# Moving the weight parts of the x-stationary products by 64 bytes, and one order for the products of all summed units

## Chip, cores and metric

The kernel runs on one core of one Trainium2 chip. The metric is device time in microseconds (us) of one execution, the median of the runs shown. Engines are named as the profile names them: PE (matrix products; PEld is its weight load), DVE and ACT (elementwise work), POOL and SP (here mostly issuing DMAs).

## The reference

Two layers over 256 tokens with 1024 features, all in float32. Each layer is a feed-forward block, a mixing block and a second feed-forward block; the first lines below are the whole of it.

```python
def swiglu(h, w_gate_up, w_down):
    a, b = jnp.split(h @ w_gate_up, 2, axis=-1)
    return (jax.nn.silu(a) * b) @ w_down

def hybrid_layer(x, ...):
    x = x + 0.5 * swiglu(rms_norm(x, ffn1_norm), ffn1_w_gate_up, ffn1_w_down)
    h = rms_norm(x, mix_norm)
    z = h @ w_in
    ...
    u, q, k, v, gl = z[..., :o1], z[..., o1:o2], z[..., o2:o3], z[..., o3:o4], z[..., o4:]
    ...
    merged = gates[:, :, 0] * (y_pool @ w_branch_pool) + gates[:, :, 1] * (y_attn @ w_branch_attn)
    x = x + merged @ w_out
    x = x + 0.5 * swiglu(rms_norm(x, ffn2_norm), ffn2_w_gate_up, ffn2_w_down)
    return x
```

y_pool is a causal pooling of u, and y_attn is attention over q, k and v. The sizes that matter: w_in has 4096 columns, the hidden width of a feed-forward block is 2816.

## The kernel before

**Parts and products.** A float32 product is made of three products of float32r parts: each operand is split into a high part, which ACT writes as a copy (lines 198, 209, 319), and a low part, which DVE writes as the difference (lines 199, 210, 320). High times high, high times low and low times high are added in PSUM; low times low is left out. `steps` (line 218) reorders the columns of the moving operand and of the output in pieces of 16 bytes.

**Units of weights.** All weights come as units of 128 x 2048 floats (1 MB). `fetch` (line 134) takes the next unit of a plan, issues its DMA on SP into one of four `raw` tiles, and has its two halves split into two `hi` and two `lo` tiles of 128 x 1024, from a pool with six buffers of each name (`buffers`, line 202). The unit then waits in a list until `unit` (line 128) hands it to the products.

**Weights stationary.** In most stages the weight block is the stationary operand and x, or what was made from x, moves: `chain` (line 228) multiplies a high weight block with the high and low x parts side by side (512 columns) and then the low weight block with the high x part (256 columns). `pair` (line 246) does this for one unit: eight blocks of features, two outputs, 32 products. The x parts are in the tile hx, one pair of 256 columns for each block of 128 features.

**x stationary.** Two places turn this round: a block of 128 features of x for 128 tokens is stationary, and the weights move.

- `tokens` (line 686) makes q, k and v: three calls in a layer, each over two units of w_in, and for each half of the tokens. For each block of features it does four products: high x with 512 high weight columns, high x with the first 256 low columns, low x with 512 high columns, and high x with the last 256 low columns. The stationary blocks are slices of hx.
- `by_tokens` (line 555) does the same for **summed units**. In three of the four feed-forward blocks (all but the very first) some products by the gate and up weights are made in Strassen's manner: seven products of sums of quadrants take the place of eight. Form 1 to 7 of a group A, B or C is called "1A", "7C" and so on. The sums of weights are formed in HBM beforehand by accumulating DMAs from POOL (`go_on`, line 175), loaded by `sum_form` (line 187) and split like any unit. Of x, forms 1, 2 and 4 use quadrants of hx themselves; forms 3, 5, 6 and 7 use sums of quadrants, which `x_forms` (line 525) makes and splits into the tile sf. Forms 1, 2 and 4 thus have slices of hx stationary, the others slices of sf.

Each summed unit is 16 products: four blocks of 128 features with four products each. A forms list, TWO or THREE (lines 54 and 56), is the order in which a feed-forward block takes plain units (numbers, each a `pair`), summed units and the transposes "t0A" and the like, which turn a finished result back. The first block after the mixing block of layer 0 uses TWO, the two feed-forward blocks of layer 1 use THREE. Runs of summed units, such as "4A", "2B", "3A", "7B", "6B" in THREE, follow one another without a `pair` between.

**The order of the work.** Products stay on PE in the order in which the code writes them (`keep`, line 107). In `by_tokens` the four products of a block are written in two ways: for forms 3, 5, 6 and 7 as in `tokens` (512, 256, 512, 256 columns), for forms 1, 2 and 4 as 512, 512, 256, 256.

**Addresses.** A tile's place follows from the sizes of those ahead of it. In the program before, all `hi` and `lo` tiles begin at 32 modulo 128 bytes, and so do hx, ga, gb, gc and gd (the moving operands of the feed-forward blocks). Only the parts in sf begin 64 bytes further (SHIFT is 16 floats, line 49; `eight`, line 396), at 96 modulo 128. A block's own offsets are multiples of 512 bytes.

Of the kernel before, what the change touches and what calls it, by code (L numbers as in the profile page):

```python
# [19 lines left out]
F32R = mybir.dt.float32r  # L20
# [5 lines left out]
P = 128  # L26
# [5 lines left out]
NF = DFF // P  # L32
# [6 lines left out]
HALF = 8 * P  # L39
# [6 lines left out]
LU = FU + NF + NF // 2  # L46
GROUPS = {"A": 12, "B": 8, "C": 18}
XF = 2
SHIFT = 16
# [29 lines left out]
def trunk_kernel(ctx: ExitStack, tc: tile.TileContext, x_in, w_in, pw_in, qkn_in, rope_in, mask_in, band_in, out):  # L79
# [4 lines left out]
    parts = ctx.enter_context(tc.tile_pool(name="parts", bufs=6))  # L84
# [24 lines left out]
    def mm(*args, **kw):  # L109
        return keep(nc.tensor.matmul(*args, **kw))  # L110
# [17 lines left out]
    def unit():  # L128

        if not ahead:  # L130
            fetch()
        return ahead.pop(0)

    def fetch(last=None):

        u = next(plan)
        if isinstance(u, tuple):
            ahead.append(sum_form(*u))
            return
        raw, hi, lo = buffers()  # L140
        n = HALF if u < 4 else 2 * HALF
        for c in range(0, 2 * HALF, n):
            nc.sync.dma_start(raw[:, c:c + n], w_in[u, :, c:c + n])
        for h in range(2):
            low = split(raw[:, h * HALF:(h + 1) * HALF], hi[h], lo[h])
        if last:
            behind(low, last)
        ahead.append((hi, lo))
# [3 lines left out]
    def quadrant(base, g, q):  # L152

        n, kh = base + GROUPS[g] + (0 if q[1] == "1" else 2), int(q[0]) - 1
        return w_in[n:n + 2, :, kh * HALF:(kh + 1) * HALF].rearrange("u p c -> p u c")

    def two_rows(z):
        return z.rearrange("p (i c) -> p i c", i=2)
# [28 lines left out]
    def sum_form(base, n):  # L187

        f, g = n
        z, hi, lo = buffers()  # L190
        src = quadrant(base, g, RAW[f]) if f in RAW else two_rows(far.pop((f, g, base)))
        z = two_rows(z)
        nc.sync.dma_start(z, src)
        z = z.rearrange("p i (k c) -> p i k c", c=2 * P)
        for h in range(2):
            a = z[:, :, 2 * h:2 * h + 2, :]
            hv, lv = (t[h].rearrange("p (k i c) -> p i k c", i=2, c=2 * P) for t in (hi, lo))
            act(hv, a, AF.Copy)  # L198
            tt(lv, a, hv.bitcast(F32), op=OP.subtract)  # L199
        return hi, lo  # L200

    def buffers():
        raw = raws.tile([P, 2 * HALF], F32, name="raw", tag="raw")
        hi = [parts.tile([P, HALF], F32R, name="hi", tag="hi") for _ in range(2)]
        lo = [parts.tile([P, HALF], F32R, name="lo", tag="lo") for _ in range(2)]
        return raw, hi, lo

    def split(w, hi, lo):
        act(hi, w, AF.Copy)  # L209
        return tt(lo, w, hi.bitcast(F32), op=OP.subtract)  # L210

    def blk(z, b, n=1):

        size = z[0].shape[-1]
        c = b * P % size
        return z[b * P // size][:, c:c + n * P]

    def steps(z):

        if len(z.shape) == 3:  # L220
            z = z.rearrange("p a s -> p (a s)")
        return z.rearrange("p (s a c) -> p a s c", a=4, c=4)

    def prod(ps, w, xk, first, last, **kw):

        return mm(steps(ps), lhsT=w, rhs=steps(xk), start=first, stop=last, **kw)
# [35 lines left out]
    def behind(z, other):  # L262

        tc.add_manual_dep(z.ins, other.ins.name, mybir.DependencyInfo(
            mybir.DependencyClass.NoSync, mybir.DependencyReason.DATA), reason="behind")
# [130 lines left out]
    def eight(dtype, name, at=0):  # L396
        z = acts.tile([P, NK * GW + 4 * SHIFT], dtype, name=name, tag="gates")[:, at:]
        return [z[:, i * GW:(i + 1) * GW] for i in range(NK)]
# [21 lines left out]
    def ffn(after, n0=0, end=False, col=None, base=0, far_at=(), steps_at=()):  # L420
        gs, gt = {}, {}

        def room(name, n0, m):
            g = acts.tile([P, m, 2, S], F32R, name=name, tag=name)
            gt[name] = g
            gs.update({n0 + i: g[:, i] for i in range(m)})
# [9 lines left out]
        abs_, more = {}, []  # L436
# [40 lines left out]
        if n0:  # L477
            room("gb", 16, NF - 16)
            ws = [unit() for _ in range(n0)]
            pairs(ws, [wide(n) for n in range(n0)])  # L480
            pair(unit(), wide(n0), sums, NK // 2)
            fetch()
            done = 0
            for i in range(n0 + 1, NF + 1):
                if i < NF:
                    pair(unit(), wide(i))
                    fetch()
                    if i in (7,9,11,13,15,17,19,21):
                        go_on()
                if i == NF or i % 3 != 1:  # L490
                    for n in range(done, NF if i == NF else min(done + 2, i - 1), 2):
                        scaled = post(n)
                        done = n + 2
                        if i == n0 + 1:
                            behind(scaled, drained[-1])
        else:
# [24 lines left out]
            sf = {}  # L521
# [3 lines left out]
            def x_forms():  # L525

                late = drained[-1]
                for k in range(NK):
                    behind(act(xg[:, k, :], x[:, k, :], AF.Copy, scale=gain[:, l_of[0], col + k:col + k + 1]), late)
                (a11, a21), (a12, a22) = ([z[:, :, t * P:(t + 1) * P] for t in range(2)] for z in (xg[:, :4], xg[:, 4:]))  # L530
                s1, s2 = (pre[:, (8 + 2 * i) * S:(10 + 2 * i) * S].rearrange("p (k s) -> p k s", s=P) for i in range(2))
                s3, s4 = (vt[:, i, :].rearrange("p (k s) -> p k s", s=P) for i in range(2))
                fs = iter(eight(F32R, "sf", SHIFT))

                def parts_of(n, z):
                    sh, sl = (next(fs).rearrange("p (k s) -> p k s", s=P) for _ in range(2))
                    act(sh, z, AF.Copy)
                    tt(sl, z, sh.bitcast(F32), op=OP.subtract)
                    sf[n] = [(sh[:, k, :], sl[:, k, :]) for k in range(4)]

                tt(s3, a11, a21, op=OP.subtract)
                parts_of("7", s3)
                yield
                tt(s1, a22, a21, op=OP.subtract)
                stt(s2, s1, -1.0, a11, op0=OP.mult, op1=OP.subtract)
                parts_of("6", s2)
                yield
                parts_of("5", s1)
                yield
                stt(s4, s2, -1.0, a12, op0=OP.mult, op1=OP.subtract)  # L550
                parts_of("3", s4)
                room("gb", 16, NF - 16)
                yield

            def by_tokens(f, ps, first):

                hi, lo = unit()
                more = {} if first else {"skip_group_check": True}
                for k, (ah, al) in enumerate(sf[f]):
                    wh, wl = blk(hi, 4 * k, 4), blk(lo, 4 * k, 4)  # L560
                    low = ps[:, :S], ah, wl[:, :S], False, False
                    prod(ps, ah, wh, first and k == 0, False, **more)
                    if f not in "124":
                        prod(*low, **more)
                    prod(ps, al, wh, False, False, **more)
                    if f in "124":
                        prod(*low, **more)
                    prod(ps[:, S:], ah, wl[:, S:], False, k == 3, **more)
                fetch()

# [23 lines left out]
            def seven(f, g):  # L594

                z = bank[f + g]
                p1, w = tk[g][:, 0], tk[g][:, 1]
                if f == "5":
                    if g == "B":
                        gated(p1, 0, 0, 0)  # L600
                    if three and g == "C":
                        p1 = tk["B"][:, 0]
                by_tokens(f, z, f in "127")
                if f == "1":
                    act(p1, z, AF.Copy)
                elif f == "2":
                    tt(p1, z, p1, op=OP.add)
                    if g != "B":
                        gated(p1, 0, 0, 0)
                elif f == "6":  # L610
                    act(w, z, AF.Copy)
                elif f == "5":
                    act(p1, z, AF.Copy)
                    tt(p1, bank["7" + g], p1, op=OP.add)
                    gated(p1, 1, 1, 1)
                elif f == "3":
                    gated(z, 0, 1, 1)
                elif f == "4":
                    tt(w, z, w, op=OP.add)
                    gated(w, 1, 0, 0)  # L620
# [5 lines left out]
            for n in FEED[base][2:]:  # L626
# [4 lines left out]
                n, t = n if isinstance(n, tuple) else (n, None)  # L631
# [16 lines left out]
        for f, k in order:  # L648
            u, c = divmod(f * NF + k, 16)
# [4 lines left out]
            hi, lo = parts_of[u]  # L654
# [382 lines left out]
    for f in range(0, NK, 2):  # L1037
# [3 lines left out]
        for u, (raw, hi, lo) in enumerate(w3):  # L1041
            nc.sync.dma_start(raw[:, 2 * f * P:2 * (f + 2) * P], w_in[u, :, 2 * f * P:2 * (f + 2) * P])
            n = 1 if f == 0 else 2
# [114 lines left out]
```

## Time and profile before

| | |
|---|---|
| runs of the kernel | 994.24, 994.9 and 995.12 us, median 994.9 |
| profiled execution, span from first to last instruction | 991.9 us |
| rest, by which the median is longer than that span | 3.0 us |
| instructions in the span | 16162 |
| products on PE | 6296 |
| DMA traffic | 285.19 MB, mean 288 GB/s |

The profiled execution has no time of its own beside its span; what lies around the span is taken as the difference to the median. In the rows of the profile, "L110" is the line of a helper through which nearly all products go, so that they are told apart by the names of their tiles: "b<-hi,hx" is a product into a PSUM bank named b with hx and hi as operands. A row of the timeline begins with the start and the duration in us, and "x2" stands for two equal instructions in succession. Durations of products overlap, since they are pipelined: the spacing of two starts is what a product takes from the whole.

### The profile page before, as it was taken

How to read it: one execution, taken by the hardware profiler on the slowest of the kernel's cores; microseconds unless marked ns; L12 is line 12 of the kernel's file. 1: busy time of each engine (PE TensorE's matmuls, PEld its weight loads, DVE VectorE, ACT ScalarE, POOL GpSimd, SP SyncE). 2: the span in 40 equal slices, each digit the busy share in tenths (PEclk: the TensorE clock that was granted, in tenths of full speed). 3: DMA queues.
4: the chain of work that ended last, by engine and by line, in shares of the span. 5: the costliest groups of instructions: out<-in, count | busy, mean ns of one | idle time of the engine just before them, and what ended most of it. 6: DMA issues, size and time to landing. Idle time of an engine off the chain costs nothing.

```text
span 991.9 us, 16162 instructions
## 1 busy us (share of the span) xinstructions
PE 986.1 (99%) x6296; PEld 895.4 (90%) x6296; DVE 811.2 (82%) x1154; ACT 661.6 (67%) x988; POOL 71.0 (7%) x111
## 2 busy tenths in 40 slices
PE   9999999999999999999999999999999999999998
PEld 8989888898899988889888889988988998888897
DVE  6987777698978798886779999776988887999872
ACT  7865555567766787775578877555677568887641
POOL 0000010104100000000000000000141000000000
PEclk9999999999999999999999999999999999999999
DMA  8889899989979769899979989898799998988840
GB/s 298 322 297 323 254 327 343 309 241 292 323 237 328 255 242 324 297 325 286 311 267 305 321 289 347 277 311 279 258 298 372 248 306 299 320 314 292 293 150 22
DMA packets 50269, 285.19 MB, mean 288 GB/s; under 512 B 4753, under 2 KB 6033, under 8 KB 27409
## 3 DMA queue, kind: packets, MB, share of 16 engines
q1 hardware_dynamic: 36624, 217.05, 58.8%
q0 software_dynamic: 13568, 67.11, 27.7%
q8 instruction: 49, 0.80, 0.3%
q14 instruction: 28, 0.22, 0.1%
HBM read 283.10 MB, written 68.16 MB: 354 GB/s over the span
## 4 chain that ended last, share of the span: by engine, by line
PE 99%; DMA 0%; DVE 0%; ACT 0%; SPq 0%; issue 0%
PE ps L110 68%; PE b L110 15%; PE pt L110 7%; PE two L110 4%; PE pe L110 1%; PE sc L110 1%; PE pt L780 1%; PE y L110 1%; PE b L588 0%; DMA raw<-w 0%; PE tp L736 0%; PE pt L588 0%; PE st L110 0%; PE ss L110 0%; DVE t L681 0%; ACT hi L209 0%
## 5 line engine op out<-in xcount | busy, mean ns | idle before, releaser
L210 DVE TENSOR_TENSOR lo<-raw,hi 128x1024 fp32r<-128x1024 f32 (+2 forms) x303 | 360.9, 1203 | 104.3 <-ACT hi L209 102.9
L209 ACT ACTIVATE hi<-raw 128x1024 fp32r<-128x1024 f32 (+2 forms) x303 | 310.6, 1033 | 194.8 <-PE ps L110 123.1
L110 PE MATMUL ps<-hx,hi 128*128 128x512 f32 x1184 | 400.2, 384 | 0.6 <-ACT hi L209 0.6
L110 PE MATMUL ps<-hx,lo 128*128 128x256 f32 x1184 | 323.7, 273 | 0.0
L110 PEld LDWEIGHTS ps<-hx,hi 128*128 128x128 f32 x1184 | 222.2, 188 | 40.7 <-ACT hi L209 0.8
L110 PEld LDWEIGHTS ps<-hx,lo 128*128 128x128 f32 x1184 | 222.5, 188 | 0.3 <-DVE lo L210 0.3
L199 DVE TENSOR_TENSOR lo<-raw,hi 128x1024 fp32r<-128x1024 f32 x112 | 135.0, 1220 | 17.7 <-ACT hi L198 17.5
L198 ACT ACTIVATE hi<-raw 128x1024 fp32r<-128x1024 f32 x112 | 117.5, 1056 | 41.4 <-PE ps L110 25.3
L110 PE MATMUL ps<-ga,hi 128*128 128x512 f32 (+1 forms) x264 | 87.8, 378 | 0.0
L110 PE MATMUL b<-hi,sf 128*128 128x512 f32 x256 | 87.4, 383 | 0.0
L183 POOL DMA_DIRECT2D f<-w x48 | 44.6, 932 | 557.7 <-DVE ab L259 239.4
L110 PE MATMUL b<-lo,sf 128*128 128x256 f32 x256 | 70.2, 274 | 0.0
L110 PE MATMUL ps<-ga,lo 128*128 128x256 f32 x256 | 69.9, 273 | 0.0
L110 PE MATMUL ps<-gb,hi 128*128 128x512 f32 (+1 forms) x198 | 65.4, 376 | 0.0
L110 PE MATMUL pt<-hi,hx 128*128 128x512 f32 x192 | 64.9, 384 | 0.0
L110 PE MATMUL b<-hi,hx 128*128 128x512 f32 x192 | 59.1, 388 | 0.0
L110 PEld LDWEIGHTS ps<-ga,hi 128*128 128x128 f32 x264 | 49.0, 188 | 8.2
L110 PEld LDWEIGHTS b<-hi,sf 128*128 128x128 f32 x256 | 48.0, 188 | 8.4
L110 PE MATMUL pt<-lo,hx 128*128 128x256 f32 x192 | 52.5, 274 | 0.0
L110 PE MATMUL ps<-gb,lo 128*128 128x256 f32 x192 | 52.4, 273 | 0.0
L110 PEld LDWEIGHTS ps<-ga,lo 128*128 128x128 f32 x256 | 48.1, 188 | 0.0
L110 PEld LDWEIGHTS b<-lo,sf 128*128 128x128 f32 x256 | 48.0, 188 | 0.0
(209 smaller groups left out, 1590.6 us busy)
## 6 DMA issues: line engine op xcount, KB each, us to landing
raw<-w SPq DMA_DIRECT2D x168, 1024.0 KB, 7.2
f<-w POOLq DMA_DIRECT2D x48, 1024.0 KB, 11.9
raw<-f SPq DMA_DIRECT2D x32, 1024.0 KB, 5.8
raw<-w SPq DMA_DIRECT2D x16, 256.0 KB, 5.3
out_dram<-gx SPq DMA_DIRECT2D x8, 128.0 KB, 1.9
gx<-x SPq DMA_DIRECT2D x3, 256.0 KB, 5.5
qk<-pw SPq DMA_DIRECT2D x2, 256.0 KB, 5.7
gx<-x SPq DMA_DIRECT2D x1, 300.0 KB, 2.8
```

Of the source, the lines that this page charges most:

```text
L110: return keep(nc.tensor.matmul(*args, **kw))
L183: z = nc.gpsimd.dma_start(two_rows(far[f, g, base]), src, **kw)
L198: act(hv, a, AF.Copy)
L199: tt(lv, a, hv.bitcast(F32), op=OP.subtract)
L209: act(hi, w, AF.Copy)
L210: return tt(lo, w, hi.bitcast(F32), op=OP.subtract)
L780: keep(nc.tensor.transpose(pt[:, h, o * P:(o + 1) * P], pr[:, h, c * P:(c + 1) * P], ident))
```

## The change

It has two parts.

**Place.** `buffers` makes each `hi` and `lo` tile 32 floats (128 bytes) longer, and hands out 1024 floats of it from an offset: 16 floats (64 bytes) for the summed units and for the first six units after a feed-forward block's 33, which are those of `tokens`, and 0 for all others. The parts in sf, before 64 bytes from the start of their tile, now lie 128 bytes from it. So in both x-stationary places the weights begin at 96 modulo 128 bytes; hx stays at 32, and sf is at 32 now. Before, the distance was 0 for hx and 64 for sf; now it is 64 for both. Because the twelve `hi` and `lo` tiles are longer, they begin 4224 instead of 4096 bytes apart, and the tiles behind them lie 1536 bytes further; with the weights stationary the distance to the x parts is still 0 modulo 128, but takes both values modulo 256.

**Order.** `by_tokens` writes the four products of a block in one way for all forms: 512, 256, 512, 256 columns.

```diff
-        raw, hi, lo = buffers()
+        t = (u - NF - NF // 2) % LU
+        raw, hi, lo = buffers(SHIFT if t < 6 else 0)
...
     def sum_form(base, n):
 
         f, g = n
-        z, hi, lo = buffers()
+        z, hi, lo = buffers(SHIFT)
...
-    def buffers():
+    def buffers(at=0):
         raw = raws.tile([P, 2 * HALF], F32, name="raw", tag="raw")
-        hi = [parts.tile([P, HALF], F32R, name="hi", tag="hi") for _ in range(2)]
-        lo = [parts.tile([P, HALF], F32R, name="lo", tag="lo") for _ in range(2)]
+        hi, lo = ([parts.tile([P, HALF + 2 * SHIFT], F32R, name=n, tag=n)[:, at:at + HALF] for _ in range(2)]
+                  for n in ("hi", "lo"))
         return raw, hi, lo
...
-                fs = iter(eight(F32R, "sf", SHIFT))
+                fs = iter(eight(F32R, "sf", 2 * SHIFT))
...
                     prod(ps, ah, wh, first and k == 0, False, **more)
-                    if f not in "124":
-                        prod(*low, **more)
+                    prod(*low, **more)
                     prod(ps, al, wh, False, False, **more)
-                    if f in "124":
-                        prod(*low, **more)
                     prod(ps[:, S:], ah, wl[:, S:], False, k == 3, **more)
```

On PE, at the first summed unit of TWO ("1A", into the bank b0, right behind a `pair` that ends with the tile lo_3488), the program before has these rows; hi_3601 and lo_3603 are the parts of the first half of the unit's weights:

```order
L110 MATMUL ps_3495<-hx_126,hi_3486 128x4x32x4
L110 MATMUL ps_3495<-hx_126,lo_3488 128x4x16x4
L110 MATMUL b0_3596<-hi_3601,hx_126 128x4x32x4 x2
L110 MATMUL b0_3596<-lo_3603,hx_126 128x4x16x4 x2
L110 MATMUL b0_3596<-hi_3601,hx_126 128x4x32x4 x2
```

The changed program has these in the same place:

```order
L110 MATMUL ps_3495<-hx_126,hi_3486 128x4x32x4
L110 MATMUL ps_3495<-hx_126,lo_3488 128x4x16x4
L110 MATMUL b0_3596<-hi_3601,hx_126 128x4x32x4
L110 MATMUL b0_3596<-lo_3603,hx_126 128x4x16x4
L110 MATMUL b0_3596<-hi_3601,hx_126 128x4x32x4
L110 MATMUL b0_3596<-lo_3603,hx_126 128x4x16x4
```

The second 512-column product and the first 256-column product of each block have changed places: the low part is read by the second product instead of the third.

The second place on PE is where an hx unit hands over to an sf unit inside a run of THREE ("2B" into b1, then "3A" into b2). Before:

```order
L110 MATMUL b1_5316<-lo_5780,hx_126 128x4x16x4 x2
L110 MATMUL b1_5316<-hi_5778,hx_126 128x4x32x4 x2
L110 MATMUL b1_5316<-lo_5780,hx_126 128x4x16x4 x2
L110 MATMUL b2_5317<-hi_5807,sf_5413 128x4x32x4
L110 MATMUL b2_5317<-lo_5809,sf_5413 128x4x16x4
```

Changed:

```order
L110 MATMUL b1_5316<-hi_5778,hx_126 128x4x32x4
L110 MATMUL b1_5316<-lo_5780,hx_126 128x4x16x4
L110 MATMUL b1_5316<-hi_5778,hx_126 128x4x32x4
L110 MATMUL b1_5316<-lo_5780,hx_126 128x4x16x4
L110 MATMUL b2_5317<-hi_5807,sf_5413 128x4x32x4
L110 MATMUL b2_5317<-lo_5809,sf_5413 128x4x16x4
```

The hx unit now ends with the same alternation with which the sf unit begins, where before it ended with two 256-column products. No other instruction of PE moves, and the instructions of DVE, ACT, POOL and SP stand in the same order as before.

## The prediction

> **What bounds the kernel now.** I read the page's busy times and chain first, then PE's waits, then PE's products by form, and last the timeline around single units.
>
> ```profile
> PE 986.1 (99%) x6296; PEld 895.4 (90%) x6296; DVE 811.2 (82%) x1154; ACT 661.6 (67%) x988; POOL 71.0 (7%) x111
> PEclk9999999999999999999999999999999999999999
> PE 99%; DMA 0%; DVE 0%; ACT 0%; SPq 0%; issue 0%
> ```
>
> PE is busy from end to end, at the full granted clock in every slice, and the chain that ended last is PE alone. The list of PE's waits has two rows:
>
> ```profile
> PE busy L110 <- DVE eps L298: 1.1, 1, 1.1
> PE ps L110 <- ACT hi L209: 0.6, 1, 0.6
> ```
>
> PE waits 1.7 us in all, at the start. So the time is the sum of the spacings, start to start, of 6296 products, and a change of placement or order can act only through these spacings. The durations in the form groups overlap and are not the spacing; the groups serve as counts.
>
> ```profile
> L110 PE MATMUL ps<-hx,hi 128*128 128x512 f32 x1184 | 400.2, 384 | 0.6 <-ACT hi L209 0.6
> L110 PE MATMUL b<-hi,sf 128*128 128x512 f32 x256 | 87.4, 383 | 0.0
> L110 PE MATMUL pt<-hi,hx 128*128 128x512 f32 x192 | 64.9, 384 | 0.0
> L110 PE MATMUL b<-hi,hx 128*128 128x512 f32 x192 | 59.1, 388 | 0.0
> ```
>
> The products that the diff names are the last three groups, with as many 256-column ones beside them. I count them in **groups of sixteen**: eight products of 512 columns and eight of 256, which is one summed unit, or one half of the tokens over one w_in unit. 256/8 = 32 summed units have an sf form stationary, 192/8 = 24 have hx itself, and `tokens` has 192/8 = 24 groups, four to a call. The rest, such as the first row, keeps the weights stationary.
>
> All forms do the same 6144 columns in a group, yet take different times. The timeline gives each by the difference of two starts. Weights stationary, eight pairs in a row:
>
> ```profile
> 341.13 0.38 PE L110 MATMUL ps<-hx,hi 128*128 128x512 f32 x1
> 343.80 0.38 PE L110 MATMUL ps<-hx,hi 128*128 128x512 f32 x1
> ```
>
> That is 2.67 us. Now the summed units; here the first row of each unit, and of what follows it. The first is an sf unit that follows a pair with the weights stationary:
>
> ```profile
> 374.26 0.38 PE L110 MATMUL b<-hi,sf 128*128 128x512 f32 x1
> 376.95 0.38 PE L110 MATMUL ps<-hx,hi 128*128 128x512 f32 x1
> ...
> 553.69 0.61 PE L110 MATMUL b<-hi,hx 128*128 128x512 f32 x2
> 556.42 0.62 PE L110 MATMUL b<-hi,hx 128*128 128x512 f32 x2
> 559.18 0.38 PE L110 MATMUL b<-hi,sf 128*128 128x512 f32 x1
> 561.86 0.38 PE L110 MATMUL b<-hi,sf 128*128 128x512 f32 x1
> 564.53 0.38 PE L110 MATMUL b<-hi,sf 128*128 128x512 f32 x1
> 567.20 0.38 PE L110 MATMUL ps<-hx,hi 128*128 128x512 f32 x1
> ```
>
> The sf unit after a pair takes 2.69. The second piece is the run 4A, 2B, 3A, 7B, 6B of THREE: hx after a pair 2.73, hx after hx 2.76, sf after hx 2.68, sf after sf 2.67 and 2.67. The "x2" on the hx rows is the old order: two 512-column products together. The other neighbourhoods (2C, 3C, 4C after an sf unit; 3A of TWO; 1C of TWO and 5B of THREE behind four transposes):
>
> ```profile
> 603.90 0.62 PE L110 MATMUL b<-hi,hx 128*128 128x512 f32 x2
> 606.59 0.39 PE L110 MATMUL b<-hi,sf 128*128 128x512 f32 x1
> 609.31 0.62 PE L110 MATMUL b<-hi,hx 128*128 128x512 f32 x2
> 612.01 0.39 PE L110 MATMUL ps<-ga,hi 128*128 128x512 f32 x1
> ...
> 385.02 0.38 PE L110 MATMUL b<-hi,sf 128*128 128x512 f32 x1
> 387.73 0.39 PE L110 MATMUL ps<-hx,hi 128*128 128x512 f32 x1
> ...
> 393.44 0.69 PE L110 MATMUL b<-hi,hx 128*128 128x512 f32 x2
> 396.29 0.39 PE L110 MATMUL ps<-hx,hi 128*128 128x512 f32 x1
> ...
> 573.34 0.47 PE L110 MATMUL b<-hi,sf 128*128 128x512 f32 x1
> 576.10 0.38 PE L110 MATMUL ps<-hx,hi 128*128 128x512 f32 x1
> ```
>
> hx after sf 2.69 and 2.70, sf after such an hx unit 2.72 and 2.71, hx after transposes 2.85, sf after transposes 2.76. The price of a unit thus depends on its neighbour, and hx units cost most. Last, the first `tokens` call of each layer (four groups each, ended by the "ones,acc" products):
>
> ```profile
> 182.08 0.40 PE L110 MATMUL pt<-hi,hx 128*128 128x512 f32 x1
> 184.80 0.38 PE L110 MATMUL pt<-hi,hx 128*128 128x512 f32 x1
> 192.80 0.50 PE L110 MATMUL st<-ones,acc 128*128 128x1 f32 x4
> ...
> 671.58 0.39 PE L110 MATMUL pt<-hi,hx 128*128 128x512 f32 x1
> 674.33 0.39 PE L110 MATMUL pt<-hi,hx 128*128 128x512 f32 x1
> 682.54 0.50 PE L110 MATMUL st<-ones,acc 128*128 128x1 f32 x4
> ```
>
> In layer 0 the first group takes 2.72 and the other three 8.00/3 = 2.67 each. In layer 1 the same program takes 10.96 for four, 2.74 each: with this placement and the alternating order there are two states, a quick one and a slow one, and a call can stay in the slow one. The sf units, 64 bytes apart from their weights, fall back to 2.67 after at most one unit.
>
> **The change part by part.** *Order.* In 24 hx units, four times each, 512-512-256-256 becomes 512-256-512-256, the order of the sf units. Nothing is added or removed. *Place.* Summed and `tokens` units have their parts 64 bytes on, and sf moves on by 64 as well: sf to weights stays 64 bytes apart, hx to weights goes from 0 to 64 (modulo 128). So every group with x stationary gets what the sf units have now, and I price each by an sf unit in the same neighbourhood:
>
> - 13 hx units after a pair (1A, 2A, 4A, 2C, 4C of TWO; 1A, 2A, 4A, 1C of THREE, twice): 2.73 to 2.69, and a little less where the unit took 2.72: 13 x 0.035 = 0.46 us.
> - 6 hx after hx (1B, 2B, 4B, twice): 2.76 to 2.67, 0.54.
> - 4 hx after sf (2C, 4C of THREE, twice): 2.695 to 2.67, 0.10.
> - 1 hx after transposes (1C of TWO): 2.85 to 2.76, 0.09.
> - 8 sf units after hx (3A and 3C of TWO; 3A, 3B, 3C of THREE, twice), where the neighbour now hands over in step: two at 2.71, four at 2.68, two at 2.72, all to 2.67: 0.08 + 0.04 + 0.10 = 0.22.
> - `tokens`: layer 1's first call goes to layer 0's pace, 10.96 to 10.72: 0.24. The five other calls I put at no change.
>
> The sum is 1.65 us, all on PE and so all on the path. Unknown is what 64 bytes do to `tokens` and to an hx unit, neither of which the trace shows in that place. Below, the nearest row is 2.67 for every group: 0.02 more on the 13 + 12 units after a pair, 0.05 on the first group of each layer's first call, 0.6 in all; the gain is then 2.25. Above, it is layer 1's 2.74 for every group, taken as a rival. I take the sf prices, since these are the same instructions at the same distance.
>
> *Longer tiles.* Twelve buffers (six hi, six lo) grow by 128 bytes, and the tiles behind them move by multiples of 128; where the weights are stationary they stay 0 from their x parts modulo 128, but no longer always the same modulo 256. I cost this at nothing: in the program before, hx and ga lie at different distances from the weights modulo 512, and the pairs that read either have 384 ns:
>
> ```profile
> L110 PE MATMUL ps<-ga,hi 128*128 128x512 f32 x248 | 85.0, 384 | 0.0
> ```
>
> *An earlier need.* The second product of an hx unit now reads the low part, which DVE makes, one 512-column product (about 0.23 us) sooner. The sf units have that order, and the waits list has no wait for DVE's lo; if the cover were gone it would cost at most 24 x 0.23 = 5.5 us. ACT, DVE, POOL and SP keep their instructions in the same order.
>
> One page speaks against any effect. The Trainium skill ("TensorE: Matmul & The Clock Gate", Back-to-back issue gap) gives an isolated warm gap of columns/2.4 plus 2.5 ns, whatever the order and the addresses. An estimate from it is 6144/2.4 + 16 x 2.5 = 2.60 us for every group, and a gain of zero. Here groups of equal columns take 2.67 to 2.85, so the trace does not follow it.
>
> **The rivals.**
> 1. *Neither order nor place sets the pace:* the extra time belongs to the switch of stationary operand, and hx units stay at 2.72 to 2.76. No change, 994.9. Against it: the same hx parts run at 2.67 in `tokens`. It is what the page above would give.
> 2. *Order alone acts:* the first five terms hold, 1.41, without `tokens`: 993.5. For it: `tokens` reaches 2.67 at distance 0. The Trainium skill ("SBUF — State Buffer", Who interferes with whom) gives PE separate read ports for the moving operand and the weights, by which place would not matter; the slow and the quick call at one placement neither bear that out nor refute it.
> 3. *More than priced:* 64 bytes also take away the slow starts: 2.25, 992.65, or 0.09 more on each of five units if the 2.76 behind transposes goes too, 992.2: about 992.4. For it: sf after sf shows 2.67 without any start cost.
> 4. *The slow state takes over,* slower than before: in the new place the x-stationary groups sit at layer 1's 2.74 as that call does. Then 8 sf units go from 2.67 (+0.56), 12 from 2.69 (+0.60), 8 from 2.69 on average (+0.40), five `tokens` calls from 2.68 (20 x 0.06 = +1.20), and hx units, whose present mean is (13 x 2.725 + 6 x 2.76 + 4 x 2.695 + 2.85)/24 = 2.73, +0.2: in all 3.0, 997.9. It decides once the 80 groups on average take longer than today; 0.025 us each make the 2.0 us that a measurement shows. Against it: sf units leave that state.
> 5. *The longer tiles bring the weight-stationary pairs into it:* half of 1184/8 = 148 groups, at +0.07: 5.2, 1000.1. The equal rows of hx and ga speak against it.
>
> **How the numbers follow.** The span is 991.9, the median of the runs 994.9 (994.24 to 995.12); the 3.0 around the span should not move. The forecast is 994.9 - 1.65 = 993.25, so 993.2, span about 990.2. Chances: forecast 0.50, rival 1 0.10, rival 2 0.13, rival 3 0.19, rival 4 0.05, rival 5 0.03. A measurement tells about 0.2% apart, 2.0 us, and my sum lies just inside. Faster by more: rival 3 and a third of the forecast, whose sum needs only 0.35 more (the runs differ by 0.9): 0.36. Slower: rivals 4 and 5, 0.08. Within: 0.56. The range runs from rival 3 less half the runs' spread, 991.7, to rival 1 plus it, 995.4.
>
> **What would show it.** Right: b rows without "x2"; hx units after a pair at 2.69, hx after hx at 2.67, the unit after hx at 2.67; layer 1's first call at about 10.72; weight-stationary eights still 2.67; no new row in PE's waits. Wrong: hx units at 2.72 or more in the new order (rival 1), `tokens` groups at 2.74 (rival 4), weight-stationary eights off 2.67 (rival 5), or a PE wait for DVE's lo.

## The result and the profile after

The changed kernel takes 1003.74 us (median of 4 runs, 1003.49 to 1005.25), the kernel before 994.57 us (median of 4 runs beside it): a ratio of 1.0094 [1.0079, 1.0108], slower by 9.2 us. Its profiled execution has a span of 1001.7 us and took 1003.49 us. Of all runs behind the times below, one of e8's eleven (1256.0 us, granted clock 0.753) stands apart from the rest and is left out of its ratio. The page after, the busy times, the clock and the chain:

```profile
PE 996.2 (99%) x6296; PEld 897.7 (90%) x6296; DVE 811.4 (81%) x1154; ACT 661.6 (66%) x988; POOL 70.9 (7%) x111
PEclk9999999999999999999999999999999999999999
PE 99%; DMA 0%; DVE 0%; ACT 0%; SPq 0%; issue 0%
```

PE's busy time grew by 10.1 us with the same 6296 products; DVE, ACT and POOL stayed within 0.2 us. PE's waits after:

```profile
PE busy L110 <- DVE eps L299: 1.1, 1, 1.1
PE ps L110 <- ACT hi L210: 0.3, 1, 0.3
```

No wait is new. PE still runs without a gap at the full granted clock, so the loss lies inside the spacings. PE's products by form:

```profile
L110 PE MATMUL ps<-hx,hi 128*128 128x512 f32 x1184 | 405.5, 388 | 0.3 <-ACT hi L210 0.3
L110 PE MATMUL b<-hi,sf 128*128 128x512 f32 x256 | 88.1, 387 | 0.0
L110 PE MATMUL ps<-ga,hi 128*128 128x512 f32 x248 | 85.9, 388 | 0.0
L110 PE MATMUL b<-hi,hx 128*128 128x512 f32 x192 | 66.1, 387 | 0.0
L110 PE MATMUL pt<-hi,hx 128*128 128x512 f32 x192 | 65.2, 385 | 0.0
```

The forms that the diff does not name lost: the 512-column products with the weights stationary went from 384 to 388 ns, those with hx and those with ga alike. The timeline shows how. Below are the starts of four half units, of eight pairs each, and of the second its first four 512-column products:

```profile
60.19 0.38 PE L110 MATMUL ps<-hx,hi 128*128 128x512 f32 x1
...
62.85 0.40 PE L110 MATMUL ps<-hx,hi 128*128 128x512 f32 x1
63.20 0.38 PE L110 MATMUL ps<-hx,hi 128*128 128x512 f32 x1
63.54 0.40 PE L110 MATMUL ps<-hx,hi 128*128 128x512 f32 x1
63.89 0.38 PE L110 MATMUL ps<-hx,hi 128*128 128x512 f32 x1
...
65.60 0.39 PE L110 MATMUL ps<-hx,hi 128*128 128x512 f32 x1
...
68.27 0.40 PE L110 MATMUL ps<-hx,hi 128*128 128x512 f32 x1
```

The half at 60.19 takes 2.66 us, the next 2.75, the third 2.67 again: quick and slow halves side by side. In the slow one the pairs take 0.35, 0.34 and 0.35, where a half of 2.67 has 0.33 on average. I put the address of each operand (from the built program) beside its start in the trace. **Distance** from here on is the address of the stationary operand less that of the moving one, in bytes, modulo 256. The halves at 60.19 and 65.60 have distance 128, the one at 62.85 has 0.

Last, the run 4A, 2B, 3A, 7B, 6B of THREE, the first row of each unit and of the `pair` behind it, and then the first `tokens` call of layer 1:

```profile
559.92 0.40 PE L110 MATMUL b<-hi,hx 128*128 128x512 f32 x1
562.65 0.39 PE L110 MATMUL b<-hi,hx 128*128 128x512 f32 x1
565.37 0.39 PE L110 MATMUL b<-hi,sf 128*128 128x512 f32 x1
568.12 0.38 PE L110 MATMUL b<-hi,sf 128*128 128x512 f32 x1
570.81 0.38 PE L110 MATMUL b<-hi,sf 128*128 128x512 f32 x1
573.50 0.38 PE L110 MATMUL ps<-hx,hi 128*128 128x512 f32 x1
...
678.97 0.38 PE L110 MATMUL pt<-hi,hx 128*128 128x512 f32 x1
689.79 0.50 PE L110 MATMUL st<-ones,acc 128*128 128x1 f32 x4
```

The order is the new one ("x1"), but the units take 2.73, 2.72, 2.75, 2.69 and 2.69 where the forecast had 2.69 and four times 2.67. The call takes 10.82 us, about halfway from 10.96 to the forecast 10.72.

**Where the 9.8 us between the two spans lie.** The table has means, worked out from the starts in the trace, without the few that a stall broke (a pair over 400 ns, a block over 760; in e11 below also without the altered blocks). A pair is a product of 512 columns and one of 256; a block is the four products of an x-stationary block of features, a quarter of a group of sixteen:

| | before: distance, ns | after: distance, ns |
|---|---|---|
| pair, weights stationary | 128: 333.9 (x1850) | 128: 335.0 (x934); 0: 342.5 (x918) |
| block of an hx unit | 128: 682.9 | 64: 679.9; 192: 677.1 |
| block of an sf unit | 192: 672.3 | 64: 678.5; 192: 676.3 |
| block of `tokens` | 128: 672.5 | 64: 678.1; 192: 670.9 |

The pairs lose 918 x 8.6 + 934 x 1.1 ns = 8.9 us. Of the x-stationary groups, the 96 hx blocks gain 0.4, the 128 sf blocks lose 0.7 and the 96 `tokens` blocks 0.2. Together that is a loss of 8.9 - 0.4 + 0.7 + 0.2 = 9.4 of the 9.8 us.

### The profile page after: what moved, and what is told of

Same layout as the page of the kernel before. It is cut to its first block, busy times and chain, and to the rows that moved or that the text cites. A ratio compares the mean times of both kernels' runs of the same rounds, so it can differ in the third digit from the quotient of the medians.

```text
span 1001.7 us, 16162 instructions
## 1 busy us (share of the span) xinstructions
PE 996.2 (99%) x6296; PEld 897.7 (90%) x6296; DVE 811.4 (81%) x1154; ACT 661.6 (66%) x988; POOL 70.9 (7%) x111
## 4 chain that ended last, share of the span: by engine, by line
PE 99%; DMA 0%; DVE 0%; ACT 0%; SPq 0%; issue 0%
PE ps L110 68%; PE b L110 15%; PE pt L110 7%; PE two L110 4%; PE pe L110 1%; PE sc L110 1%; PE pt L778 1%; PE y L110 1%; PE b L586 0%; DMA raw<-w 0%; PE tp L734 0%; PE pt L586 0%; PE st L110 0%; PE ss L110 0%; DVE t L679 0%; ACT hi L210 0%
## 5 line engine op out<-in xcount | busy, mean ns | idle before, releaser
L110 PE MATMUL ps<-hx,hi 128*128 128x512 f32 x1184 | 405.5, 388 | 0.3 <-ACT hi L210 0.3
L110 PE MATMUL b<-hi,hx 128*128 128x512 f32 x192 | 66.1, 387 | 0.0
L110 PE MATMUL b<-lo,hx 128*128 128x256 f32 x192 | 52.7, 274 | 0.0
```

## The experiments

An expectation calls its theories by letters and says what each means for that kernel. A, in most of them, is that a product stream slows down where stationary and moving operand lie at distance 0. Every kernel was timed against the kernel before in the same call, on the same chip. The last four columns give the mean ns of a pair and of a block by distance, as in the table above.

| kernel | us, before in the same call | ratio [95%] | pairs | hx | sf | `tokens` |
|---|---|---|---|---|---|---|
| e1 | 1005.02, 994.55 | 1.0105 [1.009, 1.0121] | 128: 335.0, 0: 342.4 | 686 | 677 | 682 |
| e2 | 995.32, 994.55 | 1.0008 [0.9999, 1.0016] | 128: 334.5 | 128: 684.6 | 192: 675.3 | 128: 672.5 |
| e3 | 996.16, 994.55 | 1.0012 [1.0004, 1.0021] | 128: 334.3 | 64: 676.1 | 192: 679.1 | 64: 676.2 |
| e4 | 1005.18, 994.55 | 1.0107 [1.0092, 1.0122] | 128: 334.6, lo at 0: 342.0 | 685 | 679 | 682 |
| e5 | 1005.94, 994.26 | 1.0116 [1.0098, 1.0135] | 337.3 to 340.2 | 683 | 684 | 683 |
| e6 | 1002.65, 994.26 | 1.0084 [1.007, 1.0098] | 128: 335.3, hi at 0: 341.1 | 684 | 678 | 674 |
| e7 | 996.15, 994.26 | 1.0024 [1.0015, 1.0033] | 128: 335.7 | 192: 669.7 | 192: 669.9 | 192: 667.6 |
| e8 | 994.57, 994.26 | 1.0001 [0.9992, 1.001] | 128: 333.9 | 64: 676.2 | 192: 675.0 | 128: 675.0 |
| e9 | 1009.93, 994.31 | 1.0156 [1.014, 1.0171] | 0: 340.6 | 0: 687.6 | 64: 677.6 | 0: 681.7 |
| e10 | 997.96, 994.31 | 1.0035 [1.0022, 1.0047] | 64: 337.1 | 192: 669.1 | 192: 669.8 | 192: 667.9 |
| e11 | 996.55, 994.31 | 1.0022 [1.0013, 1.0032] | 128: 336.2 | 192: 669.6 | 192: 670.8 | 192: 667.5 |
| e12 | 996.17, 994.31 | 1.0019 [1.0009, 1.0028] | 128: 335.9 | 192: 669.6 | 192: 669.9 | 192: 667.6 |
| e13 | 999.5, 994.06 | 1.0055 [1.0034, 1.0076] | 192: 336.7 | 64: 682.8 | 192: 669.2 | 64: 676.2 |
| e14 | 993.77, 994.06 | 0.9995 [0.9986, 1.0004] | 128: 334.1 | 192: 670.5 | 192: 671.4 | 192: 667.6 |

**e1, the longer tiles alone.** The kernel before with hi and lo tiles 128 bytes longer; no offset, old order.

```diff
-        hi = [parts.tile([P, HALF], F32R, name="hi", tag="hi") for _ in range(2)]
-        lo = [parts.tile([P, HALF], F32R, name="lo", tag="lo") for _ in range(2)]
+        hi, lo = ([parts.tile([P, HALF + 2 * SHIFT], F32R, name=n, tag=n)[:, :HALF] for _ in range(2)]
+                  for n in ("hi", "lo"))
```

> The program before with hi and lo tiles 128 bytes longer, used from their start; no shift, old order. Theory A (the longer tiles put half of the weights at a distance of 0 modulo 256 bytes from the x parts, and those weight-stationary pairs take 342 ns instead of 334): about 900 pairs x 8.5 ns = 7.7 us slower than before, 1002.3. Theory B (the 64-byte place of the x-stationary weights, or the order, makes the slow pairs through the phase that it leaves): no change, 994.6, all pairs at 334.

It took 1005.02 us: the longer tiles alone make the whole loss and a little more. Half of the pairs are at 0, and those carry most of the loss: 918 x 8.5 + 933 x 1.1 ns = 8.8 us. Theory A has the cause; its 1002.3 left out the x-stationary blocks, whose distances the longer tiles change too, and which lose another 1.8 us.

**e2, the order alone.** The change's edit of `by_tokens`, and nothing else:

```diff
-                    if f not in "124":
-                        prod(*low, **more)
+                    prod(*low, **more)
                     prod(ps, al, wh, False, False, **more)
-                    if f in "124":
-                        prod(*low, **more)
```

> The program before with one order of products for all summed units, and nothing moved. Theory A: the order is harmless or good; by the first five terms of the prediction 1.4 us faster than before, 993.2. Theory B, order: some of the 9.2 us loss shows here, 996 or more.

The same run of THREE in e2's timeline:

```profile
555.11 0.39 PE L110 MATMUL b<-hi,hx 128*128 128x512 f32 x1
557.86 0.39 PE L110 MATMUL b<-hi,hx 128*128 128x512 f32 x1
560.61 0.38 PE L110 MATMUL b<-hi,sf 128*128 128x512 f32 x1
563.32 0.39 PE L110 MATMUL b<-hi,sf 128*128 128x512 f32 x1
566.04 0.38 PE L110 MATMUL b<-hi,sf 128*128 128x512 f32 x1
568.76 0.39 PE L110 MATMUL ps<-hx,hi 128*128 128x512 f32 x1
```

It reads 2.75, 2.75, 2.71, 2.72, 2.72; before it was 2.73, 2.76, 2.68, 2.67, 2.67. At the old place the hx units gain nothing from the order (684.6 against 682.9), and the sf units behind them, which are not touched, lose (675.3 against 672.3). So the pace of a unit can go over to the next. The time lies between the two theories', and its interval does not exclude no change.

**e3, the whole change with tiles 256 bytes longer.** Four small tiles get fewer buffers for room; all pairs come back to 128.

```diff
-        hi, lo = ([parts.tile([P, HALF + 2 * SHIFT], F32R, name=n, tag=n)[:, at:at + HALF] for _ in range(2)]
+        hi, lo = ([parts.tile([P, HALF + 4 * SHIFT], F32R, name=n, tag=n)[:, at:at + HALF] for _ in range(2)]
```

> The changed program with hi and lo tiles 256 bytes longer in place of 128, so that their distance to the x parts stays 128 modulo 256 for weights at offset 0; four small tags of the softmax and head-norm steps have fewer buffers to make room. Theory A: the weight-stationary pairs are all back at 334 ns, and what is left of the change is order and 64 bytes: 993.5 to 995.5. Theory B: the loss stays, about 1003.

The pairs come back as theory A says. Of the 9.2 us 1.6 are left, just over its range, and these are still a loss: hx blocks come down to 676.1 only, and `tokens` and sf blocks rise, though the sf blocks lie at 192 as before. So the change would not have gained even without its side effect. (The fewer buffers are not what costs: e8 has them too, and loses nothing.)

**e4 and e6, lo tiles alone and hi tiles alone longer.** In the kernel before, one line of the two; e4:

```diff
-        lo = [parts.tile([P, HALF], F32R, name="lo", tag="lo") for _ in range(2)]
+        lo = [parts.tile([P, HALF + 2 * SHIFT], F32R, name="lo", tag="lo")[:, :HALF] for _ in range(2)]
```

> The program before with only the lo tiles 128 bytes longer; the hi tiles stay 128 modulo 256 from the x parts, half of the lo tiles come to 0. Theory A1 (the load of a low block during the 512-column product before it is what collides): as slow as both tiles longer, about 1002. Theory A2 (the load of a high block during the 256-column product collides): near before, 995. Theory B: 994.6.

> The mirror of the run with longer lo tiles: only the hi tiles 128 bytes longer, half of the high blocks at 0 modulo 256 from the x parts, all low blocks at 128. Theory A1 (the load of the low block during the 512-column product collides): pairs at 334 whatever the high block's place, 994.6 to 996. Theory A2 (either load collides): half of the pairs at 338 or more, 999 or more.

Pairs whose lo block is at 0 take 342.0, those whose hi block is at 0 take 341.1, the others 334.6 and 335.3. Either one is enough, and both together (e1: 342.4) hardly add. The view that the high block alone, or the low one alone, does the harm fell. e6's time is in the range of A2, e4's is 3 us over A1's.

**e5, steps of 32 bytes.** As e1, but 32 bytes longer, so that distances come in steps of 32.

```diff
-        hi, lo = ([parts.tile([P, HALF + 2 * SHIFT], F32R, name=n, tag=n)[:, :HALF] for _ in range(2)]
+        hi, lo = ([parts.tile([P, HALF + SHIFT // 2], F32R, name=n, tag=n)[:, :HALF] for _ in range(2)]
```

> The program before with hi and lo tiles 32 bytes longer, used from their start: the twelve tiles lie at distances from the x parts that differ in steps of 32 bytes modulo 256. It measures the price of a weight-stationary pair by distance. Theory A (only a distance near 0 modulo 256 is slow): pairs whose low block is at 0 take about 342 ns, all others 333 to 335; one tile of six, 1900/6 x 8.5 ns = 2.7 us, 997 in all. Rival C (every step away from 128 costs something, by its size): prices between 334 and 342 at 32 to 96 and 160 to 224, and 998 to 1001 in all.

No distance has the 334 back: pairs take 337.3 to 340.2, with the hi and the lo block of a pair at two different distances (128 for one and 64 for the other: 340.2), and the time lies over both forecasts. That 0 alone is bad fell. No pair here has both blocks at 128; in the runs so far only such pairs take 334.

**e9, e10 and e13, every weight tile at one distance.** Unused bytes behind the input tile push all later tiles on: 128, 64 and 192 bytes; sf is placed as in the row of the table; e10 has the new order too.

```diff
-    gx = acts.tile([P, L * NG + NK * S + 8], F32, name="gx")
+    gx = acts.tile([P, L * NG + NK * S + 8 + 2 * SHIFT], F32, name="gx")
```

> The program before with 128 unused bytes behind the input tile, so that hx and all tiles behind it move and every weight tile, not half of them, lies 0 modulo 256 from the x parts; old order, nothing else. Theory A (distance 0 costs 8.5 ns per weight-stationary pair): all 1900 pairs at 342, 16 us slower, 1010. Theory F (a mixture of distances costs, one distance for all lets the pairs settle): pairs at 334, 994 to 996.

> The program before with 64 unused bytes behind the input tile, the sf parts at their tile's start and one order: all x parts, hx, sf and those of the down products alike, lie 192 modulo 256 beyond their weights, without longer weight tiles. Theory C (a weight-stationary pair is quick at 128 alone): pairs at 339 to 340 as in the run with 32-byte steps, x-stationary groups at 667, 1003 in all. Theory F: pairs at 334 and groups at 667, 992.5.

> The program before with 192 unused bytes behind the input tile and the sf parts 128 bytes into their tile: the weights lie 192 modulo 256 beyond the x parts for all weight-stationary products, so that the table of one distance for all (128, 64, 0) gets its fourth value; hx lies 64 beyond its weights where it is stationary, sf 192 as before; old order. By symmetry with 64 (337.3 ns): pairs at 337, 998 to 1000 in all. If only 0 is slow: pairs at 334, 994 to 996.

In e9 no weight tile is longer; its only edit is the line above. The same halves of eight pairs:

```profile
61.12 0.39 PE L110 MATMUL ps<-hx,hi 128*128 128x512 f32 x1
63.84 0.39 PE L110 MATMUL ps<-hx,hi 128*128 128x512 f32 x1
66.56 0.39 PE L110 MATMUL ps<-hx,hi 128*128 128x512 f32 x1
69.28 0.39 PE L110 MATMUL ps<-hx,hi 128*128 128x512 f32 x1
```

Every half takes 2.72, and the kernel 15.6 us more, as theory A says. With the old tiles e9 is slow, with the longest e3 is quick (334.3): what matters is not the length or the spacing of the tiles, but the distance. A pair takes 333.9 ns in the kernel before, all at 128, 337.1 in e10, all at 64, 336.7 in e13, all at 192, and 340.6 in e9. e13's 999.5 lies in the range forecast from the symmetry with 64. e10 at 997.96 met neither forecast: its blocks (667.9 to 669.8) come near the 667 of both, its pairs lie between the two.

**e7, the x-stationary groups all at 192.** Against e3:

```diff
-        raw, hi, lo = buffers(SHIFT if t < 6 else 0)
+        raw, hi, lo = buffers(3 * SHIFT if t < 6 else 0)
...
-        z, hi, lo = buffers(SHIFT)
+        z, hi, lo = buffers(3 * SHIFT)
...
-                fs = iter(eight(F32R, "sf", 2 * SHIFT))
+                fs = iter(eight(F32R, "sf", 0))
```

> As the run with 256 bytes longer tiles, but the x-stationary weights 192 bytes on and the sf parts at their tile's start: x lies 192 modulo 256 beyond its weights for hx and sf alike, which is the distance of sf before. Theory D (the pace of x-stationary groups goes by the distance, and 192 has the quick state of sf before, 2.67 to 2.69): hx and sf units near 671 ns for four products, 1.2 us less for hx, 993.4. Theory E (the pace goes by what the neighbours leave behind, and no one place is quick): groups at 675 to 680, 995 to 996.

```profile
555.47 0.38 PE L110 MATMUL b<-hi,hx 128*128 128x512 f32 x1
558.15 0.38 PE L110 MATMUL b<-hi,hx 128*128 128x512 f32 x1
560.81 0.38 PE L110 MATMUL b<-hi,sf 128*128 128x512 f32 x1
563.48 0.38 PE L110 MATMUL b<-hi,sf 128*128 128x512 f32 x1
566.15 0.38 PE L110 MATMUL b<-hi,sf 128*128 128x512 f32 x1
568.81 0.38 PE L110 MATMUL ps<-hx,hi 128*128 128x512 f32 x1
571.55 0.39 PE L110 MATMUL ps<-hx,hi 128*128 128x512 f32 x1
```

Here are the paces of the prediction, or better: 2.68, 2.66, 2.67, 2.67, 2.66. By the means the x-stationary blocks gain 96 x 13.2 + 128 x 2.4 + 96 x 4.9 ns = 2.0 us. But the half of the `pair` behind the run, at distance 128 like before, takes 2.74 where it took 2.68: over 1849 pairs the mean rises by 1.8 ns, 3.3 us. What the run gains, the pairs behind it give back, and more: theory D's paces came, its 993.4 us did not. In e10 x lies elsewhere and the weights are where they were, but the distance is 192 too, and the blocks have the same means within 0.6 ns: it is the distance that sets them, not either address.

**e8, only the hx units moved.** Against e3: the weights of forms 1, 2 and 4 alone get the 64 bytes.

```diff
-        raw, hi, lo = buffers(SHIFT if t < 6 else 0)
+        raw, hi, lo = buffers()
...
-        z, hi, lo = buffers(SHIFT)
+        z, hi, lo = buffers(SHIFT if f in "124" else 0)
...
-                fs = iter(eight(F32R, "sf", 2 * SHIFT))
+                fs = iter(eight(F32R, "sf", SHIFT))
```

> As the run with 256 bytes longer tiles, but only the weights of forms 1, 2 and 4 are moved by 64 bytes; sf, its weights and the weights of tokens stay as in the program before; one order. Theory D: hx groups at 676 as in that run, sf groups back at 671, tokens at 671: 0.6 us under before, 994.0. Theory E: sf groups stay at 678 because of the hx units around them: 995.

hx blocks gain 6.7 ns (0.6 us), sf and `tokens` blocks lose 2.7 and 2.5 (0.6 us), and pairs stay: no change, 994.57. The sf blocks at 675.0 lie between theory D's 671 and theory E's 678, and the time lies between theirs.

**e11, e12 and e14: what hands the slow pace over.** All on e7. e11 writes the last block of a run as 512, 256, 256, 512; e12 writes it in the old order; e14 leaves the run alone and writes the first block of features of the `pair` behind it as 512, 512, 256, 256. The core of e11, then of e12, then of e14:

```diff
+                    if at_end and k == 3:
+                        prod(ps[:, S:], ah, wl[:, S:], False, False, **more)
+                        prod(ps, al, wh, False, True, **more)
+                        continue
...
+                    if at_end and k == 3:
+                        prod(ps, al, wh, False, False, **more)
+                        prod(*low, **more)
...
+            if kick and kick.pop():
+                for part in range(2):
+                    for j in range(2):
+                        if part == 0:
+                            prod(ps[:, j], blk(w[0], 2 * k + j), hk[k], k == 0, False)
+                        else:
+                            prod(ps[:, j][:, 0, :], blk(w[1], 2 * k + j), hk[k][:, 0, :], False, False)
+                continue
```

> As the run with the weights 192 bytes on; in the last block of a summed unit that a pair or transposes follow, the order is 512, 256, 256, 512, so that the run ends with a 512-column product. Theory G (the slow pairs behind a run of summed units, 146 ns for 16 pairs there, are a state that the last products hand over): the pairs behind runs come back to 334, 3 us less, 992 to 993. If the state does not depend on the last products: 996 as there.

> As the run before it in this list, but the last block of such a unit has the old order of the hx forms, 512, 512, 256, 256. Theory G: the pairs behind runs change their state, 992 to 993 if it is the quick one; if the state does not depend on the last products: 996.

> As the run with the x-stationary weights 192 bytes on, but the first feature block of the first pair behind a run of summed units has its four products as 512, 512, 256, 256. Theory G (a slow state that is kept until something else than a pair comes): the kick ends it, the 146 ns for 16 pairs behind each run become about 30, some 3 us less, 992.5 to 993.5, faster than the program before. If the kick leads back into the same state, or the slow pairs come from elsewhere: 996.

In e11 and e12 the pairs behind the runs stay slow: the sixteen take 137 and 146 ns more than at 333.4 each, against 146 in e7. In e14 this is gone (about 20), as its timeline behind the run shows:

```profile
565.98 0.38 PE L110 MATMUL b<-hi,sf 128*128 128x512 f32 x1
568.64 0.60 PE L110 MATMUL ps<-hx,hi 128*128 128x512 f32 x2
...
571.34 0.38 PE L110 MATMUL ps<-hx,hi 128*128 128x512 f32 x1
...
573.67 0.38 PE L110 MATMUL ps<-hx,hi 128*128 128x512 f32 x1
```

The half behind the run takes 2.70 instead of e7's 2.74, and in the next one seven pairs take 2.33, 0.333 each; the run still has its quick pace. So products at the same distance have two paces, which they keep until an irregular block breaks them: e7's pairs are slow not by their own distance but by something that the run leaves behind. The order of the run's last block is not it (e11, e12). Three runs end in down products, where e14 alters no block: two leave slow pairs, the third quick ones. The last two of these three are the same forms in the same order, in the two feed-forward blocks of layer 1; behind the first the half takes 2.74, behind the second 2.69:

```profile
613.24 0.38 PE L110 MATMUL ps<-ga,hi 128*128 128x512 f32 x1
615.98 0.39 PE L110 MATMUL ps<-gc,hi 128*128 128x512 f32 x1
...
928.48 0.39 PE L110 MATMUL ps<-ga,hi 128*128 128x512 f32 x1
931.17 0.38 PE L110 MATMUL ps<-gc,hi 128*128 128x512 f32 x1
```

The last eight blocks of the run itself take 665 to 667 ns the first time and 677 to 682 the second: here the units at the quicker pace leave pairs at the slower one, and the other way round. In the kernel before, pairs at the quicker pace stand behind units at the quicker pace too (the half at 567.20, 2.68, behind sf units of 2.67), so this is no rule; what hands the pace over stays open. e14 takes 993.77 us. Its ratio to the kernel before is 0.9995 [0.9986, 1.0004], where e7 had 1.0024: the block brings back what e7 lost, but the forecast 992.5 to 993.5, faster than before, was not reached; no difference from the kernel before can be told.

## Why the prediction was wrong

**The step that failed** is "Longer tiles": "I cost this at nothing". The argument was that hx and ga lie at different distances modulo 512 and have equal rows. Both lay at 128 modulo 256, so those rows compared places 256 bytes apart, and the change makes a difference of 128, of which the program before had no example. That row could not bound the term, and it should have been left open upwards. Measured, it is 8.9 us in the profiled pairs, and e1 with that part alone took 10.5 us more than before. Rival 5 had the place: half of the weight-stationary pairs slower. Its price of 0.07 us a group agrees with the measured 8 x 8.6 ns = 0.07 by luck, for it was taken from the slow `tokens` call, which is at distance 128 and not at 0. And it counted the 148 groups that read hx and not those that read ga, gb, gc and gd: 918 slow pairs instead of 592. It had 0.03 of the chance for the sake of the row that tested something else.

**Hx units priced by sf units: wrong too.** The terms 0.46 + 0.54 + 0.10 + 0.09 took the order and "64 apart" as what makes an sf unit quick. e2 shows that the order alone, at the old place, brings nothing. The place counts modulo 256, not 128: sf units had distance 192, and the changed hx units have 64 or 192; hx blocks take 676.1 and 676.2 at 64 (e3, e8) and 669.7 at 192 (e7). With all at 192 the gain on the x-stationary blocks is there: 1.27 us of hx, 0.31 of sf and 0.47 of `tokens`, where the prediction had 1.19, 0.22 and 0.24. So the terms fit a change that the diff does not make, and even there the pairs behind the runs take the gain away. Whether the order has a part in it at the new place is not shown: every run with hx units at 192 has the new order, and at 64 the old order (e13) gives 682.8, but among other neighbours.

**Sf units behind hx and `tokens`: wrong in sign.** In place of 0.22 and 0.24 us of gain, sf blocks lost 0.7 and `tokens` blocks 0.2 us. Half of them came to 64 and lost about 6 ns each. Of those that stayed at 192 or came there, the sf blocks lost 4 ns, which their own distance does not explain (in e2 and e3, too, sf blocks stay at 192 and lose, 675.3 and 679.1, beside changed neighbours); the `tokens` blocks gained 1.6.

**An earlier need of lo: right.** No wait for DVE's lo came up.

**Time as a sum of spacings: right**, and it led straight to the place. The remainder around the span was not: the prediction had 3.0 us, the changed kernel's execution has 1003.49 - 1001.7 = 1.8, and in every run on record the time is 1.7 to 1.9 us longer than the span. So the execution profiled before was one of the quicker ones, not the median.

**An estimate by columns alone, and the ports.** An estimate from the isolated gap that the Trainium skill gives ("TensorE: Matmul & The Clock Gate", Back-to-back issue gap) is 512/2.4 + 2.5 + 256/2.4 + 2.5 = 325 ns for a pair, with no address in it. Measured are 334 to 342, by distance, so the measurement decides. The Trainium skill ("SBUF — State Buffer", Who interferes with whom) calls PE's read ports for the moving operand and for the weights independent. The runs do not bear out what the prediction drew from that, that place would not matter: e9 moves addresses alone and takes 1.56% more. Whether the ports have a part in it is not shown.

## What to carry over

Where PE is busy from end to end, the relative address of weights and moving operand can be a part of the time, here 334 to 342 ns for the same pair: before adding padding to a pool, work out where every later tile comes to lie, modulo 256 at least, and not only the tiles that the edit is for. A row can bound a term only if it differs in what the edit changes. And the price of a group in a stream of products belongs to its neighbours as well: measure a stage together with what stands behind it.

## What the runs showed beside that

- **A pace by address.** For these products a pair takes 333.9 ns with all at distance 128, 337.1 at 64, 336.7 at 192 and 340.6 at 0 (among other neighbours up to 336.2 at 128 and 342.5 at 0, in e11 and the changed kernel), with a granted clock of 0.999 or 1.0. With x stationary, a block takes 667.6 to 669.9 where all lie at 192 (e7 and e10), and 676 to 683 at 64 (e3, e8 and e13); but among slower neighbours sf blocks at 192 take 679.1 (e3). What in the chip depends on the distance stays open: no run here looks inside PE or the memory. The runs also cannot tell whether it counts from the moving operand to the weights of its own product or to those of the next one, since the blocks lie multiples of 512 bytes apart.
- **Two paces at one distance,** handed on by what went before: 2.74 and 2.69 us for the same half in two places of e14, and 335.7 and 334.1 ns over all pairs of e7 and e14.
- **A start at half pace in some executions.** The first pairs of e14's profiled execution:

```profile
6.78 0.63 PE L110 MATMUL ps<-hx,hi 128*128 128x512 f32 x1
7.21 0.41 PE L110 MATMUL ps<-hx,lo 128*128 128x256 f32 x1
7.42 0.63 PE L110 MATMUL ps<-hx,hi 128*128 128x512 f32 x1
...
9.74 0.39 PE L110 MATMUL ps<-hx,hi 128*128 128x512 f32 x1
9.97 0.28 PE L110 MATMUL ps<-hx,lo 128*128 128x256 f32 x1
10.09 0.38 PE L110 MATMUL ps<-hx,hi 128*128 128x512 f32 x1
```

A pair takes 0.64 us up to 9.3 us, 0.40 at 9.34, and 0.35 and less afterwards, though the clock column of that stretch reads 1.00. In the execution profiled before, pairs take 0.33 from the second on, and at 10.4 us e14 is 1.9 us behind it, of which 0.45 were lost before the first pair. The Trainium skill ("TensorE: Matmul & The Clock Gate", Part 1: The HAM clock gate) has 512 columns at 426.7 ns on a cold array, and says that the number of cold products differs from run to run. The 0.43 from 6.78 to 7.21 agrees, and e4's profiled execution has such a start too, by one pair longer. How often it comes, and how much of the spread of a kernel's times is due to it, no run here shows.
